# A decoder layer on one core: the third pair of k tiles by seven products in two more stages, and a last group cut further

## The chip, the core and the metric

The kernel runs on one core of one Trainium2 chip, in one launch. The metric is the device time of an execution in microseconds; the times below are medians of three runs. TensorE (PE) does the matmuls, VectorE (DVE) and ScalarE (ACT) the element work, and SyncE (SP) issues the transfers of weights.

## What is computed

One layer of a decoder for 256 tokens and a width of 2048, everything in float32: a gated linear recurrence and an attention side by side, a gated feed-forward block, and a gated embedding at the end. Cut to the products that matter here:

```python
h = rmsnorm(x, g_mix[i])
x_r, g_r, q, k, v, gate_r, gate_a = jnp.split(h @ w_in[i], IN_SPLIT_POINTS, axis=-1)
y_r = (gelu(g_r) * rg_lru(conv(x_r), ...)) @ w_rnn_out[i]
y_a = stick_breaking_attention(norm(q), norm(k), v) @ w_attn_out[i]
x = x + (sigmoid(gate_r) * y_r + sigmoid(gate_a) * y_a) @ w_o[i]
g, u = jnp.split(rmsnorm(x, g_ffn[i]) @ w_ffn_gu[i], 2, axis=-1)
x = x + (silu(g) * u) @ w_ffn_down[i]
ple_gate = sigmoid(rmsnorm(x, g_ple[i]) @ w_ple_gate[i])
x = x + ple_gate * (p[i] @ w_ple_proj[i])
```

The stages that use them are called ro (`w_rnn_out`), v (its columns of `w_in`), ao, wo, gu, dn (`w_ffn_down`, in three parts) and pg (`w_ple_gate`, with `p @ w_ple_proj` inside, which the kernel calls embedded).

## The kernel before

**Products.** Each float32 operand is kept as two parts, hi and lo. A product (`prod`, lines 573 to 575) is three matmuls into one PSUM bank: tokens' hi by weights' hi, hi by lo, lo by hi. The tokens (128 x 128) are what PE loads, 512 columns of weights are what it streams.

**Groups.** The function `group` runs one wide group: 256 tokens by 1024 output columns, as four quarters of 128 tokens by 512 columns, which lie in four PSUM banks called "2", "4", "3" and "8", with a fifth, "B". v and pg have two groups each, g = 0 and 1. A list of slots says what the group does in order. A number is one tile of 128 rows of weights: four products, one for each quarter. Two neighbouring tiles (a pair) can be done with seven products rather than eight, from sums of the four weight blocks and of the token blocks (Strassen's scheme in Winograd's form). The strings "11", "T1", "21", "22", "T2", "T3", "T4" are such slots, and each serves two pairs at a time. `("S", i, 2)`, i from 1 to 4, are the seven products of a third pair. `SEVEN` has two pairs (62 products), `SEVEN3` three (61). Before, only gu uses `SEVEN3`.

**Weights.** `Stream` loads chunks of 512 KB by SP (line 257), plain ones into a ring of four buffers (the profile's w), blocks for sums into Q tiles. SP issues in program order; a plain chunk has to wait until a buffer's wlo has been made. ACT copies the hi part (line 307, whi), DVE subtracts for the lo part (line 308, wlo), chunk by chunk, some four chunks ahead of PE. Where a slot needs a sum, `summed` has DVE add first: a 1024-wide add (line 291) for T1 to T4; for the third pair two 512-wide adds (line 266) for S2 and one each for S3 and S4, which have no transfer of their own.

**Order.** The program is recorded and then put in order by a scheduler, engine by engine, on a simulated timeline. Each engine then runs its instructions in that order and waits on semaphores. Most DVE work is seen in the profile under the helpers' lines: 381 (`tt`, an add or product of two tensors), 384 (`stt`, with a scalar), ACT's under 387 (`actv`).

**Around the change.** The first v group follows the last ro group; its results are read from the banks by DVE and scaled (line 384) while the second v group starts. pg,0 follows the second group of dn's third part, from whose banks DVE adds to the residual x1 (line 381); the sums of squares and the turned tiles (line 1091, small transposes on PE) for the last norm come from these. In the last group (pg,1) the last three k tiles are done quarter by quarter, so that the quarters end one after the other and the gate, the product and the last add run while PE still works; the last quarter's gate is done in two halves of 256 columns.

Of the kernel before, what the change touches and what calls it, by code (L numbers as in the profile page):

```python
# [48 lines left out]
def pairs_of(name):  # L49

    if name[:2] == "dn":
        q = int(name[2])
        return [FQ0[q] // 2 + i for i in range(2 if FQ[q] == 16 else 1)]
    return (0, 1, 2) if name == "gu" else (0, 1)


def is_sum(x):
# [104 lines left out]
def tail():  # L162


    def wide(name, w, slots, c=0):
        return [(name, g, w, c + 8 * g, c + 8 * g + 4, slots[g]) for g in range(2)]

    def blocks(*cs):
        return [("blk", b, None, c, None, None) for c, b in cs]

    def gu(*gs):
        return [("gu", g, "gu", 4 * g, 44 + 4 * g, SEVEN3) for g in gs]

    def dn(q):
        k, p = FQ0[q], FQ0[q] // 2
        slots = [x if isinstance(x, str) else x + k for x in SEVEN] if FQ[q] == 16 else [
            x if isinstance(x, int) else x + (p,) for x in ONE(k)]
        return wide(f"dn{q}", "dn", [slots] * 2)

    x = [("x", 0), ("x", 1)]  # L180
    return (wide("ro", "ro", [LONG] * 2) + wide("v", "in", [SEVEN] * 2, C_V)
            + blocks(*[(c, b) for b in range(4) for c in (C_Q, C_K)], *[(C_GTA, b) for b in range(4)])
            + wide("ao", "ao", [SEVEN] * 2) + wide("wo", "wo", [SEVEN] * 2) + gu(0, 1, 2, 3) + dn(0) + gu(4, 5, 6, 7) + dn(1)
            + gu(8, 9, 10) + dn(2)
            + wide("pg", "pg", [SEVEN[:-3] + x + SEVEN[-3:]] * 2))


HEAD = [("gtr", 0, "in", C_GTR, C_GTR + 4, list(range(KD)))]
# [165 lines left out]
def tile_hybrid_block(ctx: ExitStack, tc: tile.TileContext, xT: bass.AP, x: bass.AP, pT: bass.AP,  # L354
# [285 lines left out]
    def group(at, pairs, sums, after=None, also=()):  # L640
# [6 lines left out]
        name, g = at  # L647
        slots = [x for n, y, _, _, _, sl in HEAD + TAIL if (n, y) == at for x in sl
                 if isinstance(x, int) or is_sum(x)]
        seq = [(n, q) for n, x in enumerate(slots) for q in products(x, pairs_of(name)[:2])]  # L650
        if at == LAST_GROUP:
            k = len(slots) - 3
            rest = [q for q in seq if q[0] >= k]
            seq = [q for q in seq if q[0] < k] + [q for b in "2438" for q in rest if q[1][0] == b]
        first, last = {}, {}
        for i, (_, (b, y, _, _)) in enumerate(seq):
            first.setdefault(b, i)
            last[b] = i
            if y in ("11", "T1", "T2", "T3"):
                last[y] = i  # L660
        plain8 = [i for i, (_, (b, y, _, _)) in enumerate(seq) if b == "8" and not isinstance(y, str)]
        assert "11" not in last or last["T1"] < plain8[0]
        banks, tile_, got = {}, {}, {}
        for i, (n, (b, y, p, c)) in enumerate(seq):
            if n not in got:
                if n in also:
                    also[n]()
# [8 lines left out]
            else:  # L676
# [1 line left out]
                     "T1": sums[p][0], "T2": sums[p][1], "T3": sums[p][2],  # L678
                     "T4": tok(pairs, 2 * p + 1, 1)}[y]
            _, _, hi, lo, w0 = got[n].columns(c)  # L680
            s = slice(w0, w0 + 512)
            prod(ps, o, hi[:, s], lo[:, s], i == first[b], i in (last[b], last.get(y)),
                 b in "B8")
            if y in ("11", "T1", "T2", "T3") and i == last[y]:
                t = tile_[y] = tl("T")
                actv(t, ps, AF.Copy)
                if y == "T2":
                    tt(tile_["T1"], tile_["T1"], t, ALU.subtract)
                if y == "T3" and after is not None:
                    after(tile_)  # L690
        return [banks[b] for b in "2438"], tile_


# [186 lines left out]

    n = len(LONG)
    for g in range(2):
        also = {n - 2 + i: (lambda p: lambda: parts_sums(xg, xsum, p))(p) for i, p in enumerate(pairs_of("v"))} if g else {
            8: last_gate, 12: next_table}
        for i, c in enumerate(whole(("ro", g), y, ysum, also)):
            o = gtr[2 * g + i // 2][i % 2]
            tt(o, c, o, ALU.mult)
# [291 lines left out]
    def embedded(g):  # L1179
        def run():  # L1180
            for b in range(2):
                w_ = S_.take(("tok", "pg", g, ("x", b)))[0]
                for t in range(2):
                    ps = psum()
                    for k in range(2):
                        s = slice(k * 512, k * 512 + 512)
                        prod(ps, tok(pts, k, t), w_[2][:, s], w_[3][:, s], k == 0, k == 1)
                    if g == 0:
                        t_ = tl("T")
                        actv(t_, ps, AF.Copy)  # L1190
                        ps = t_
                    pp.append(ps)
        return run

    for g in range(2):
        qs_, t_ = group(("pg", g), h3, sum3, also={len(SEVEN) - 3: embedded(g)})
        for n, (q, c, op) in enumerate(zip(qs_, ("11", "T3", "T1", "T3"), (ALU.add,) * 3 + (ALU.subtract,))):
            t, b = n % 2, 2 * g + n // 2
            c, ps, o = t_[c], pp.pop(0), tl("T")
            m = 512 if g == 0 or n < 3 else 256  # L1200
            for i in range(0, 512, m):
                s = slice(i, i + m)
                tt(o[:, s], q[:, s], c[:, s], op)
                actv(o[:, s], o[:, s], AF.Sigmoid, scale=rs2[:, t:t + 1])
                tt(o[:, s], ps[:, s], o[:, s], ALU.mult)
                tt(o[:, s], o[:, s], x1[t][b][:, s], ALU.add)
                nc.sync.dma_start(out[t * P:t * P + P, b * 512 + i:b * 512 + i + m], o[:, s])
    assert S_.pos == len(PLAN)


# [59 lines left out]
```

## Time and profile before

| | us |
|---|---|
| median of 3 runs | 1873.09 (1872.94 to 1874.22) |
| the profiled execution | 1875.14 |
| its span in the profile | 1873.4 |
| first v group, first matmul to that of the next | 507.70 to 549.63 |
| second v group, first matmul | 549.86 |
| pg,0, first matmul | 1769.18 |
| pg,1, first matmul to last | 1818.71 to 1866.08 |
| last instruction of DVE ends | 1869.92 |
| SP's wait for the last output ends | 1872.30 |

The span runs from the profiled execution's first instruction to its last; the execution's own time has 1.7 us around it. A row of the timeline gives a start, a length, the engine, the line, the operation, out<-in by the program's names, and in brackets how long the engine stood idle before and what released it. Matmuls overlap in the pipeline, so a matmul is listed with 0.39 us though the next starts 0.227 us after it.

### The profile page before, as it was taken

The numbers are of one execution on the slowest core, as the hardware profiler recorded it, in microseconds if no ns is written. First come the engines' busy times: TensorE is split into PE (matmuls) and PEld (weight loads), VectorE is DVE, ScalarE is ACT, GpSimd is POOL, SyncE is SP. The second block draws the span as 40 slices with busy tenths as digits, with TensorE's granted clock in tenths as the row PEclk, the third lists the DMA queues.
The fourth block names the chain that finished last, engine by engine and source line by source line (L and its number), as shares of the span: only waits on it lengthen the run. The fifth ranks groups of instructions, "written<-read, shape, count | busy, mean of one in ns | idle before, by whom it ended". The sixth has DMA issues, their size and how long they took to land.

```text
span 1873.4 us, 24153 instructions
## 1 busy us (share of the span) xinstructions
PE 1863.6 (99%) x8958; PEld 1567.9 (84%) x8958; DVE 1466.3 (78%) x1777; ACT 1196.1 (64%) x1596; POOL 2.6 (0%) x9
## 2 busy tenths in 40 slices
PE   9999999999999999999999999999999999999998
PEld 7899989888888888888888888888888788888886
DVE  7688887677776576667798988887888888888876
ACT  6688888764555576677555765655556555665773
POOL 0000000000000000000000000000000000000000
PEclk9999999999999999999999999999999999999999
DMA  8556555666546554556466556466454566545554
GB/s 287 179 178 195 191 182 188 239 207 204 196 156 192 192 162 154 165 171 225 146 213 215 196 211 234 166 217 242 166 180 180 180 227 233 197 152 179 189 199 130
DMA packets 101926, 361.37 MB, mean 193 GB/s; under 512 B 11440, under 2 KB 12080, under 8 KB 101808
## 3 DMA queue, kind: packets, MB, share of 16 engines
q1 hardware_dynamic: 101664, 359.82, 56.7%
q8 instruction: 70, 1.15, 0.3%
q14 instruction: 48, 0.39, 0.1%
q10 hardware_dynamic: 144, 0.01, 0.0%
HBM read 357.69 MB, written 2.10 MB: 192 GB/s over the span
## 4 chain that ended last, share of the span: by engine, by line
PE 98%; DMA 1%; DVE 1%; issue 0%; ACT 0%; SPq 0%; DVEq 0%; ACTq 0%
PE ps L574 26%; PE ps L575 26%; PE ps L573 26%; PE ps L503 9%; PE ps L507 4%; PE ps L487 1%; PE ps L486 1%; PE ps L485 1%; PE ps L1149 1%; DMA Q<-in_w_dram 0%; DMA w<-in_w_dram 0%; PE ps L1091 0%; PE ps L930 0%; DVE H L381 0%; DVE wlo L308 0%
## 5 line engine op out<-in xcount | busy, mean ns | idle before, releaser
L308 DVE TENSOR_TENSOR wlo<-w,whi 128x1024 fp32r<-128x1024 f32 (+2 forms) x552 | 666.5, 1214 | 256.0 <-ACT whi L307 251.8
L574 PE MATMUL ps<-wlo,Q 128*128 128x512 f32 x2209 | 861.8, 390 | 0.8 <-DVE wlo L308 0.8
L575 PE MATMUL ps<-whi,Q 128*128 128x512 f32 x2209 | 859.7, 390 | 0.0
L573 PE MATMUL ps<-whi,Q 128*128 128x512 f32 x2209 | 822.1, 391 | 0.0
L307 ACT ACTIVATE whi<-w 128x1024 fp32r<-128x1024 f32 (+2 forms) x552 | 576.0, 1051 | 307.7 <-PE ps L575 259.3
L574 PEld LDWEIGHTS ps<-wlo,Q 128*128 128x128 f32 x2209 | 414.9, 188 | 86.1 <-DVE wlo L308 1.9
L573 PEld LDWEIGHTS ps<-whi,Q 128*128 128x128 f32 x2209 | 414.4, 188 | 86.0 <-ACT H L387 0.5
L575 PEld LDWEIGHTS ps<-whi,Q 128*128 128x128 f32 x2209 | 414.7, 188 | 85.4
L307 ACT ACTIVATE whi<-Q 128x1024 fp32r<-128x1024 f32 (+1 forms) x227 | 234.7, 1036 | 238.3 <-PE ps L575 187.2
L308 DVE TENSOR_TENSOR wlo<-Q,whi 128x1024 fp32r<-128x1024 f32 (+1 forms) x227 | 270.5, 1193 | 60.6 <-ACT whi L307 58.1
L503 PE MATMUL ps<-Q,whi 128*128 128x512 f32 x704 | 170.7, 392 | 0.0
L503 PEld LDWEIGHTS ps<-Q,whi 128*128 128x128 f32 x704 | 128.7, 188 | 24.5
L291 DVE TENSOR_TENSOR Q<-Q,Q 128x1024 f32<-128x1024 f32 x100 | 122.3, 1223 | 6.3 <-DMA Q<-in_w_dram 4.6
L381 DVE TENSOR_TENSOR H<-ps,H 128x512 f32<-128x512 f32 (+1 forms) x158 | 90.3, 603 | 20.4 <-PE ps L575 13.1
L381 DVE TENSOR_TENSOR H<-H,H 128x512 f32<-128x512 f32 (+2 forms) x172 | 100.5, 600 | 7.3 <-ACT H L387 6.8
L387 ACT ACTIVATE H<-ps 128x512 f32<-128x512 f32 (+1 forms) x158 | 81.7, 533 | 37.4 <-PE ps L575 22.5
L507 PEld LDWEIGHTS ps<-Q,wlo 128*128 128x128 f32 x704 | 90.4, 191 | 3.5
L507 PE MATMUL ps<-Q,wlo 128*128 128x256 f32 x704 | 91.5, 283 | 0.0
L387 ACT ACT_TABLE_LOAD x53 | 68.0, 1283 | 1.6 <-DVE Q L381 0.7
L387 ACT ACTIVATE Q<-H 128x512 fp32r<-128x512 f32 x48 | 29.2, 624 | 26.9 <-DVE H L381 26.5
L487 PE MATMUL ps<-Q,wlo 128*128 128x256 f32 x140 | 39.6, 283 | 0.0
L486 PE MATMUL ps<-Q,whi 128*128 128x256 f32 x140 | 39.6, 283 | 0.0
(122 smaller groups left out, 883.1 us busy)
## 6 DMA issues: line engine op xcount, KB each, us to landing
w<-in_w_dram SPq DMA_DIRECT2D x530, 512.0 KB, 4.1
Q<-in_w_dram SPq DMA_DIRECT2D x126, 512.0 KB, 6.1
w<-in_w_dram SPq DMA_DIRECT2D x16, 448.0 KB, 3.4
H<-in_x_dram SPq DMA_DIRECT2D x8, 256.0 KB, 7.0
H<-in_xT_dram SPq DMA_DIRECT2D x7, 256.0 KB, 6.4
out_dram<-H SPq DMA_DIRECT2D x7, 256.0 KB, 2.8
w<-in_w_dram SPq DMA_DIRECT2D x4, 320.0 KB, 3.0
w<-in_w_dram SPq DMA_DIRECT2D x2, 256.0 KB, 3.2
```

What stands on the lines that cost most here:

```text
L291: self.nc.vector.tensor_tensor(r[o], r[o], r[a], ALU.add)
L307: self.hi_ins = self.nc.scalar.activation(hi[:, :c], t[:, :c], AF.Copy)
L308: self.lo_ins = self.nc.vector.tensor_tensor(lo[:, :c], t[:, :c], hi[:, :c].bitcast(F32), ALU.subtract)
L381: nc.vector.tensor_tensor(o, a, b, op)
L387: nc.scalar.activation(o, i, f, **kw)
L486: nc.tensor.matmul(o, wt[0], xl, start=False, stop=False)
L487: nc.tensor.matmul(o, wt[1], xh, start=False, stop=stop)
L503: nc.tensor.matmul(pss[e], wt[0], rhs(xs, k), start=(k == 0), stop=(k == n - 1))
L507: nc.tensor.matmul(pss[e][:, :256], wt[1], rhs(xs, k)[:, :256], start=False, stop=False)
L573: nc.tensor.matmul(ps, x[0], wh, start=start, stop=False, skip_group_check=goes_on)
L574: nc.tensor.matmul(ps, x[0], wl, start=False, stop=False, skip_group_check=goes_on)
L575: nc.tensor.matmul(ps, x[1], wh, start=False, stop=stop, skip_group_check=goes_on)
```

## The change

v and pg take `SEVEN3` instead of `SEVEN`: their third pair of k tiles goes by seven products instead of eight. For v, the token sums of the third pair are made in the last ro group; for pg, `next_h` makes them in the last dn group. In pg,1 the last four k tiles (before: three) go quarter by quarter, and of the last quarter these four tiles go into two new banks, 8a and 8b, of 256 columns each, one after the other; what bank 8 holds from the earlier slots is combined with its correction ahead of that, and each half is added to it. The embedded product's PSUM is copied to SBUF by ACT in both pg groups (before: in the first).

```diff
--- before.py
+++ after.py
@@ -51,7 +51,7 @@
     if name[:2] == "dn":
         q = int(name[2])
         return [FQ0[q] // 2 + i for i in range(2 if FQ[q] == 16 else 1)]
-    return (0, 1, 2) if name == "gu" else (0, 1)
+    return (0, 1, 2) if name in ("gu", "v", "pg") else (0, 1)
 
 
 def is_sum(x):
@@ -178,11 +178,11 @@
         return wide(f"dn{q}", "dn", [slots] * 2)
 
     x = [("x", 0), ("x", 1)]
-    return (wide("ro", "ro", [LONG] * 2) + wide("v", "in", [SEVEN] * 2, C_V)
+    return (wide("ro", "ro", [LONG] * 2) + wide("v", "in", [SEVEN3] * 2, C_V)
             + blocks(*[(c, b) for b in range(4) for c in (C_Q, C_K)], *[(C_GTA, b) for b in range(4)])
             + wide("ao", "ao", [SEVEN] * 2) + wide("wo", "wo", [SEVEN] * 2) + gu(0, 1, 2, 3) + dn(0) + gu(4, 5, 6, 7) + dn(1)
             + gu(8, 9, 10) + dn(2)
-            + wide("pg", "pg", [SEVEN[:-3] + x + SEVEN[-3:]] * 2))
+            + wide("pg", "pg", [SEVEN3[:-4] + x + SEVEN3[-4:]] * 2))
 
 
 HEAD = [("gtr", 0, "in", C_GTR, C_GTR + 4, list(range(KD)))]
@@ -647,21 +647,23 @@
         name, g = at
         slots = [x for n, y, _, _, _, sl in HEAD + TAIL if (n, y) == at for x in sl
                  if isinstance(x, int) or is_sum(x)]
-        seq = [(n, q) for n, x in enumerate(slots) for q in products(x, pairs_of(name)[:2])]
+        seq = [(n, q, 0, 512) for n, x in enumerate(slots) for q in products(x, pairs_of(name)[:2])]
         if at == LAST_GROUP:
-            k = len(slots) - 3
+            k = len(slots) - 4
             rest = [q for q in seq if q[0] >= k]
-            seq = [q for q in seq if q[0] < k] + [q for b in "2438" for q in rest if q[1][0] == b]
+            seq = [q for q in seq if q[0] < k] + [q for b in "243" for q in rest if q[1][0] == b]
+            seq += [(n, (b + f, *q), e, e + 256) for e, f in ((0, "a"), (256, "b")) for n, (b, *q), _, _ in rest
+                    if b == "8"]
         first, last = {}, {}
-        for i, (_, (b, y, _, _)) in enumerate(seq):
+        for i, (_, (b, y, _, _), e, _) in enumerate(seq):
             first.setdefault(b, i)
-            last[b] = i
+            last[b, e] = i
             if y in ("11", "T1", "T2", "T3"):
                 last[y] = i
-        plain8 = [i for i, (_, (b, y, _, _)) in enumerate(seq) if b == "8" and not isinstance(y, str)]
+        plain8 = [i for i, (_, (b, y, _, _), _, _) in enumerate(seq) if b == "8" and not isinstance(y, str)]
         assert "11" not in last or last["T1"] < plain8[0]
         banks, tile_, got = {}, {}, {}
-        for i, (n, (b, y, p, c)) in enumerate(seq):
+        for i, (n, (b, y, p, c), e0, e1) in enumerate(seq):
             if n not in got:
                 if n in also:
                     also[n]()
@@ -678,8 +680,8 @@
                      "T1": sums[p][0], "T2": sums[p][1], "T3": sums[p][2],
                      "T4": tok(pairs, 2 * p + 1, 1)}[y]
             _, _, hi, lo, w0 = got[n].columns(c)
-            s = slice(w0, w0 + 512)
-            prod(ps, o, hi[:, s], lo[:, s], i == first[b], i in (last[b], last.get(y)),
+            s = slice(w0 + e0, w0 + e1)
+            prod(ps[:, e0:e1], o, hi[:, s], lo[:, s], i == first[b], i in (last[b, e0], last.get(y)),
                  b in "B8")
             if y in ("11", "T1", "T2", "T3") and i == last[y]:
                 t = tile_[y] = tl("T")
@@ -688,6 +690,7 @@
                     tt(tile_["T1"], tile_["T1"], t, ALU.subtract)
                 if y == "T3" and after is not None:
                     after(tile_)
+        tile_["ends"] = [banks[b] for b in ("8a", "8b") if b in banks]
         return [banks[b] for b in "2438"], tile_
 
 
@@ -880,7 +883,7 @@
 
     n = len(LONG)
     for g in range(2):
-        also = {n - 2 + i: (lambda p: lambda: parts_sums(xg, xsum, p))(p) for i, p in enumerate(pairs_of("v"))} if g else {
+        also = {n - 3 + i: (lambda p: lambda: parts_sums(xg, xsum, p))(p) for i, p in enumerate(pairs_of("v"))} if g else {
             8: last_gate, 12: next_table}
         for i, c in enumerate(whole(("ro", g), y, ysum, also)):
             o = gtr[2 * g + i // 2][i % 2]
@@ -1185,26 +1188,29 @@
                     for k in range(2):
                         s = slice(k * 512, k * 512 + 512)
                         prod(ps, tok(pts, k, t), w_[2][:, s], w_[3][:, s], k == 0, k == 1)
-                    if g == 0:
-                        t_ = tl("T")
-                        actv(t_, ps, AF.Copy)
-                        ps = t_
-                    pp.append(ps)
+                    t_ = tl("T")
+                    actv(t_, ps, AF.Copy)
+                    pp.append(t_)
         return run
 
     for g in range(2):
-        qs_, t_ = group(("pg", g), h3, sum3, also={len(SEVEN) - 3: embedded(g)})
+        qs_, t_ = group(("pg", g), h3, sum3, also={len(SEVEN3) - 4: embedded(g)})
         for n, (q, c, op) in enumerate(zip(qs_, ("11", "T3", "T1", "T3"), (ALU.add,) * 3 + (ALU.subtract,))):
             t, b = n % 2, 2 * g + n // 2
             c, ps, o = t_[c], pp.pop(0), tl("T")
-            m = 512 if g == 0 or n < 3 else 256
-            for i in range(0, 512, m):
-                s = slice(i, i + m)
-                tt(o[:, s], q[:, s], c[:, s], op)
+            ends = t_["ends"] if n == 3 else []
+            if ends:
+                tt(c, q, c, op)
+            for i in range(0, 512, 256 if ends else 512):
+                s = slice(i, i + 256 if ends else i + 512)
+                if ends:
+                    tt(o[:, s], ends.pop(0)[:, s], c[:, s], ALU.add)
+                else:
+                    tt(o, q, c, op)
                 actv(o[:, s], o[:, s], AF.Sigmoid, scale=rs2[:, t:t + 1])
                 tt(o[:, s], ps[:, s], o[:, s], ALU.mult)
                 tt(o[:, s], o[:, s], x1[t][b][:, s], ALU.add)
-                nc.sync.dma_start(out[t * P:t * P + P, b * 512 + i:b * 512 + i + m], o[:, s])
+                nc.sync.dma_start(out[t * P:t * P + P, b * 512 + s.start:b * 512 + s.stop], o[:, s])
     assert S_.pos == len(PLAN)
```

The order moves at three places. The first is DVE at the beginning of the second v group. A name ending in a number is one tile; H are the first group's results, Q_5184 to Q_5193 what they are scaled into, Q_5199 is the sum for S2, Q_5052 and Q_5079 those for two of the T slots. Before, from the first such eviction that follows PE's end of the first group:

```order
L381 TENSOR_TENSOR H_4987<-ps_4898,H_5039 128x512
L381 TENSOR_TENSOR H_4876<-ps_4902,H_4876 128x512
L384 SCALAR_TENSOR_TENSOR Q_5166<-H_4861,rstd_tok,Q_5166 128x512
L381 TENSOR_TENSOR H_5039<-ps_4863,H_5039 128x512
L308 TENSOR_TENSOR wlo_5180<-w_215_5089,whi_5179 128x1024
L384 SCALAR_TENSOR_TENSOR Q_5169<-H_4987,rstd_tok,Q_5169 128x512
L384 SCALAR_TENSOR_TENSOR Q_5172<-H_4876,rstd_tok,Q_5172 128x512
L308 TENSOR_TENSOR wlo_5195<-Q_5107,whi_5194 128x1024
L384 SCALAR_TENSOR_TENSOR Q_5175<-H_5039,rstd_tok,Q_5175 128x512
L308 TENSOR_TENSOR wlo_5210<-w_217_5126,whi_5209 128x1024
```

and now:

```order
L381 TENSOR_TENSOR H_4956<-ps_4934,H_5050 128x512
L381 TENSOR_TENSOR H_4920<-ps_4938,H_4920 128x512
L384 SCALAR_TENSOR_TENSOR Q_5184<-H_4883,rstd_tok,Q_5184 128x512
L381 TENSOR_TENSOR H_5050<-ps_4889,H_5050 128x512
L384 SCALAR_TENSOR_TENSOR Q_5187<-H_4956,rstd_tok,Q_5187 128x512
L384 SCALAR_TENSOR_TENSOR Q_5190<-H_4920,rstd_tok,Q_5190 128x512
L266 TENSOR_TENSOR Q_5199<-Q_5070,Q_5109 128x512
L384 SCALAR_TENSOR_TENSOR Q_5193<-H_5050,rstd_tok,Q_5193 128x512
L266 TENSOR_TENSOR Q_5199<-Q_5199,Q_5109 128x512
L266 TENSOR_TENSOR Q_5109<-Q_5109 128x512
L291 TENSOR_TENSOR Q_5052<-Q_5052,Q_5197 128x1024
L291 TENSOR_TENSOR Q_5079<-Q_5079,Q_5197 128x1024
```

In the place of the lo parts between and behind the scalings there stand the three 512-wide adds of the third pair and two 1024-wide sums; the lo part of S2 (wlo_5203) and that of tile 6 follow right behind the last row.

The second is SP's queue ahead of pg,0. The Q tiles are the chunks for sums of this group, Q_15159 before and Q_15198 now being "11". Before:

```order
L257 DMA w_736_15131<-in_w_dram 128x1024
L257 DMA w_740_15204<-in_w_dram 128x1024
L257 DMA Q_15159<-in_w_dram 128x1024
L257 DMA Q_15177<-in_w_dram 128x1024
L257 DMA Q_15195<-in_w_dram 128x1024
L257 DMA Q_15240<-in_w_dram 128x1024
L257 DMA w_741_15222<-in_w_dram 128x1024
L257 DMA w_743_15259<-in_w_dram 128x1024
L257 DMA w_744_15277<-in_w_dram 128x1024
```

and now:

```order
L257 DMA w_740_15170<-in_w_dram 128x1024
L257 DMA w_746_15279<-in_w_dram 128x1024
L257 DMA w_748_15314<-in_w_dram 128x1024
L257 DMA w_750_15367<-in_w_dram 128x1024
L257 DMA Q_15198<-in_w_dram 128x1024
L257 DMA Q_15216<-in_w_dram 128x1024
L257 DMA Q_15234<-in_w_dram 128x1024
L257 DMA Q_15243<-in_w_dram 128x1024
L257 DMA Q_15261<-in_w_dram 128x1024
```

The three plain chunks that followed the four Q tiles now stand ahead of them, and the Q tiles are six.

The third is DVE at the beginning of pg,0. H_9182 to H_9188 (before: H_9152 to H_9158) are the residual x1, ps the banks of the last dn group, ssq the sums of squares; Q_15198 and Q_15234 are sums, wlo_15299 belongs to T1, wlo_15317 to 21, Q_15354 and wlo_15358 to S2. Before:

```order
L291 TENSOR_TENSOR Q_15159<-Q_15159,Q_15240 128x1024
L381 TENSOR_TENSOR H_9156<-ps_15039,H_9156 128x512
L308 TENSOR_TENSOR wlo_15280<-w_740_15204,whi_15279 128x1024
L381 TENSOR_TENSOR H_9158<-ps_15007,H_9158 128x512
L308 TENSOR_TENSOR wlo_15316<-w_741_15222,whi_15315 128x1024
L308 TENSOR_TENSOR wlo_15331<-Q_15240,whi_15330 128x1024
L308 TENSOR_TENSOR wlo_15346<-w_743_15259,whi_15345 128x1024
L384 SCALAR_TENSOR_TENSOR Q_15360<-ps_15355,prm_sb,Q_15360 128x256
```

and now:

```order
L266 TENSOR_TENSOR Q_15354<-Q_15216,Q_15261 128x512
L308 TENSOR_TENSOR wlo_15299<-Q_15198,whi_15298 128x1024
L308 TENSOR_TENSOR wlo_15317<-Q_15243,whi_15316 128x1024
L291 TENSOR_TENSOR Q_15234<-Q_15234,Q_15352 128x1024
L266 TENSOR_TENSOR Q_15354<-Q_15354,Q_15261 128x512
L266 TENSOR_TENSOR Q_15261<-Q_15261 128x512
L291 TENSOR_TENSOR Q_15198<-Q_15198,Q_15352 128x1024
L381 TENSOR_TENSOR ssq_8811<-ssq_8811 128x4
L384 SCALAR_TENSOR_TENSOR Q_15399<-ps_15394,prm_sb,Q_15399 128x256
L384 SCALAR_TENSOR_TENSOR Q_15421<-ps_15416,prm_sb,Q_15421 128x256
L384 SCALAR_TENSOR_TENSOR Q_15443<-ps_15438,prm_sb,Q_15443 128x256
L308 TENSOR_TENSOR wlo_15358<-Q_15354,whi_15357 128x1024
```

The adds to x1, of which two stood among these rows, now stand in four rows just ahead of them; three 512-wide adds and one more 1024-wide sum stand ahead of the lo part of S2.

## The prediction

> **What bounds the kernel now.** I read the page first: the busy times, the chain that ended last, the costliest groups.
>
> ```profile
> span 1873.4 us, 24153 instructions
> ...
> PE 1863.6 (99%) x8958; PEld 1567.9 (84%) x8958; DVE 1466.3 (78%) x1777; ACT 1196.1 (64%) x1596; POOL 2.6 (0%) x9
> ...
> PE 98%; DMA 1%; DVE 1%; issue 0%; ACT 0%; SPq 0%; DVEq 0%; ACTq 0%
> ...
> L574 PE MATMUL ps<-wlo,Q 128*128 128x512 f32 x2209 | 861.8, 390 | 0.8 <-DVE wlo L308 0.8
> ```
>
> TensorE is busy for 99% of the span and carries 98% of the chain. The 2209 matmuls of line 574 waited 0.8 us in all, for a wlo that DVE was late with. So a matmul taken out comes off the time, and a tile that comes late goes onto it one for one, as nothing later on PE has slack to give it back. What a matmul is worth I take from the chain, not from the 390 ns of the groups (which overlap):
>
> ```profile
> 169.50 3.65 PE ps L503 x16
> ...
> 200.48 1.91 PE ps L507 x16
> ```
>
> 16 matmuls of 512 columns take 3.65 us, 0.228 each; 16 of 256 columns 1.91, 0.119 each.
>
> The next question is how much room DVE and ACT have where the change puts work, so I read the windows of the stages: the second v group, a gate-up group (these run with three pairs already), the end of the third down projection, the first pg group.
>
> ```profile
> core 0: us, PE busy (x) PEld busy (x) DVE busy (x) ACT busy (x) POOL busy (x), PEclk, DMA share, GB/s
> 549.90:591.90 42.00, 42.00 (x187) 34.80 (x186) 29.28 (x29) 24.22 (x27) 0.00 (x0) 1.00 0.58 185
> 1108.10:1150.50 42.40, 42.40 (x192) 35.10 (x192) 37.74 (x40) 26.39 (x31) 0.00 (x0) 1.00 0.55 199
> 1735.30:1769.00 33.70, 33.70 (x158) 27.89 (x157) 28.43 (x43) 23.57 (x39) 0.00 (x0) 1.00 0.59 205
> 1769.20:1818.60 49.40, 49.40 (x227) 40.88 (x226) 38.07 (x42) 35.20 (x48) 0.00 (x0) 1.00 0.55 192
> ```
>
> The gate-up group has DVE busy for 37.74 of 42.40 us and PE without a gap: three pairs can be fed on the mean. The mean does not settle it, since a group needs its sums in its first 10 us, where DVE also empties the banks of the group before.
>
> **What is taken out.** Four groups (v and pg, two each) go from 62 to 61 products of three matmuls: 4 x 3 = 12 matmuls of 512 columns, 12 x 0.228 = **-2.74 us**. It counts in full, as PE has no gaps.
>
> **v, second group.** The sums of the third pair are new here: S2 takes two 512-wide adds (line 266), S3 one, and DVE runs in program order. By the order they now stand behind the evictions and the scalings of the first v group's results, and behind them stand two 1024-wide sums (line 291), and only then the wlo of S2. How long these take I read from the same place before:
>
> ```profile
> 549.76 1.28 DVE L381 TENSOR_TENSOR H<-ps,H 128x512 f32<-128x512 f32 x2
> 550.96 0.74 DVE L384 SCALAR_TENSOR_TENSOR Q<-H,rstd_tok,Q 128x512 fp32r<-128x512 f32 x1
> 551.62 0.69 DVE L381 TENSOR_TENSOR H<-ps,H 128x512 f32<-128x512 f32 x1
> 552.22 1.22 DVE L308 TENSOR_TENSOR wlo<-w,whi 128x1024 fp32r<-128x1024 f32 x1
> 553.35 1.41 DVE L384 SCALAR_TENSOR_TENSOR Q<-H,rstd_tok,Q 128x512 fp32r<-128x512 f32 x2
> ...
> 562.56 1.22 DVE L291 TENSOR_TENSOR Q<-Q,Q 128x1024 f32<-128x1024 f32 x1
> 563.69 1.22 DVE L308 TENSOR_TENSOR wlo<-w,whi 128x1024 fp32r<-128x1024 f32 x1
> ```
>
> From start to start: an add of 512 columns 0.60, a scaling (line 384) 0.66, a wlo 1.13, a 1024-wide sum 1.13. The first eviction at 549.76 waits for PE's last matmuls of the first group, so it cannot move. From it, in the new order, up to the wlo of S2: three evictions and four scalings (3 x 0.60 + 4 x 0.66), three 512-wide adds (1.80), two 1024-wide sums (2.26), together 8.50 us. That wlo starts at 549.76 + 8.50 = 558.26 and ends 1.22 later, 559.48. On PE the first matmul that reads it stands, in the order, 29 matmuls of 512 columns behind the group's start at 549.86: 549.86 + 29 x 0.227 = 556.44 (0.227 is what the matmuls of such a group are apart, within 1% of the 0.228). So PE must wait **3.0 us** here. (ACT's whi of S2, 1.05 us, comes behind the second add and is late too, by less.) What is queued behind on PE is the whole rest of the kernel.
>
> **v, first group.** There the adds of S2 stand ahead of the group's start, and by the same pitches wlo of S2 is ready 2.4 us before it is read. At nothing; covered by PE's matmuls on the slots ahead. Were that cover gone, it would cost as much as in the second group. The token sums of the third pair (in the last ro group for v, in dn2 for pg, a handful of short DVE adds each) lie beside PE in the same way.
>
> **pg, first group.** Here the order moves DMAs too. The chunks for sums of this group ("11" first) were issued ahead of three plain chunks on SP's queue, and now stand behind three such:
>
> ```profile
> 1754.01 1.85 SPq L257 DMA_DIRECT2D Q<-in_w_dram  x4
> 1757.38 2.60 SPq L257 DMA_DIRECT2D w<-in_w_dram  x3
> ```
>
> and for how long these 13 transfers took:
>
> ```profile
> DMA to landing us min/median/max: 3.5/6.2/8.7
> ```
>
> Such a plain chunk must wait until a wlo has freed its buffer, which at this place let the three out between 1757.38 and 1757.38 + 2.60 = 1759.98. So "11" is issued at about 1759.6 and not at 1754.01, and lands, with a landing of 4.3 us (between the least and the median of that row, as fewer transfers are queued ahead), at 1763.9. Behind it ACT's whi (1.05), then DVE goes without a gap through the order's rows: from wlo of "11" at 1765.0 to the wlo of S2 there are four wlo (4.52), three 1024-wide sums (3.39), four evictions of dn2 and three 512-wide adds (7 x 0.60 = 4.20), three scalings of 256 columns (1.2, by half of line 384's width and its fixed part) and small ones: 13.6 us. The wlo of S2 starts at 1778.6 and ends at 1779.8. On PE its reader is 29 matmuls of 512 columns and 12 small transposes behind the group's start:
>
> ```profile
> 1769.18 0.39 PE L573 MATMUL ps<-whi,Q 128*128 128x512 f32 x1
> ...
> 1774.42 0.60 PE L1091 MATMUL ps<-ident,H 128*128 128x128 f32 x4
> 1774.78 0.47 PE L574 MATMUL ps<-wlo,Q 128*128 128x512 f32 x1
> ```
>
> Four transposes move the next matmul by 0.36, 0.09 each. So it is wanted at 1769.18 + 6.58 + 1.08 = 1776.84, and PE waits **2.9 us**. From below: if "11" landed as early as before, the four evictions of dn2 would hold the row back instead, as the last of them follows PE's end of dn2 at 1769.2; from there nine rows (8.5 us) and the wlo make 1778.9, a wait of 2.1. From above: with the 8.7 us of the same row everything is 4.4 later, a wait of 7.3.
>
> **pg, second group.** Its S2 adds stand early (2.3 us after the group's start the wlo is under way, wanted 6.6 after it). At nothing.
>
> **Starting again after a wait.** The one wait of this profile shows it:
>
> ```profile
> 1494.20 0.39 PE L573 MATMUL ps<-whi,Q 128*128 128x512 f32 x1
> 1495.38 0.50 PE L574 MATMUL ps<-wlo,Q 128*128 128x512 f32 x1 [0.79 <-DVE wlo L308]
> 1495.72 0.40 PE L575 MATMUL ps<-whi,Q 128*128 128x512 f32 x1
> 1496.14 0.51 PE L573 MATMUL ps<-whi,Q 128*128 128x512 f32 x1
> 1496.49 0.40 PE L574 MATMUL ps<-wlo,Q 128*128 128x512 f32 x1
> 1496.72 0.40 PE L575 MATMUL ps<-whi,Q 128*128 128x512 f32 x1
> ```
>
> Without a wait the matmul of 1495.38 starts at 1494.43, and four matmuls later one starts at 1495.34; it started at 1496.72. Of 1.38 us, 0.95 are the wait and 0.43 the three slow matmuls behind it. I charge 0.45 for each of the two places, **+0.9**; the bounds are 0 and 1 (v's wait falls into three pieces).
>
> On the same rows a rule of the Trainium skill bears, "TensorE: Matmul & The Clock Gate", "Part 1: The HAM clock gate": after an idle window of about 3.4 us the clock is halved, and it is a busy window of that length that brings it back. The 0.79 us wait left the granted clock at 1.00 in its stage, as the rule would have it; no run here shows a longer one.
>
> **Last quarter and tail.** 12 matmuls of 512 columns become 24 of 256: 24 x 0.119 - 12 x 0.228 = +0.13, and the last one starts 0.25 later and, being half as wide, ends a little earlier. Behind it before:
>
> ```profile
> 1866.08 0.39 PE L575 MATMUL ps<-whi,Q 128*128 128x512 f32 x1
> ...
> 1866.51 1.69 DVE L381 TENSOR_TENSOR H<-ps,H 128x256 f32<-128x256 f32 x4 [0.67 <-PE ps L575]
> ...
> 1868.11 1.02 DVE L381 TENSOR_TENSOR H<-H,H 128x512 f32<-128x512 f32 x2
> 1869.04 0.42 DVE L381 TENSOR_TENSOR H<-ps,H 128x256 f32<-128x256 f32 x1
> 1869.49 0.42 DVE L381 TENSOR_TENSOR H<-H,H 128x256 f32<-128x256 f32 x1
> ```
>
> Seven DVE operations follow, the last ends 3.83 after the last matmul's start. Now the first half's operations and the subtraction stand ahead of it; but four k tiles by quarters let quarters 2 and 4 end within 0.5 us of each other, so DVE is full and takes the second half's add 0.7 after that start (before 0.43); with the same operations behind it I come to 3.17, 0.67 less. Together 0.25 - 0.67 = **-0.4**, between -0.7 (DVE in time) and 0. The four PSUM copies that ACT now makes for the embedding lie where ACT is busy for 35.20 of 49.40 us; at nothing.
>
> **The sum:** -2.74 + 3.0 + 2.9 + 0.9 - 0.4 = **+3.7 us**. The profiled execution took 1875.14 (span 1873.4 and 1.7 around it), 2.05 above the median; the sum is a difference made on its rows and stands on the median: 1873.09 + 3.7 = **1876.8**.
>
> **The rivals.**
>
> - *One wait is hidden.* DVE's evictions or the DMA of pg come earlier than I lay them. The window of dn2's end is for it (DVE 28.43 of 33.70 us, so some gaps); the eviction that waits for PE at 549.76 is against it for v. One wait with its restart less: +0.2 to +0.4, 1873.4.
> - *The change does what it says.* Gate-up runs 11 groups with three pairs and no wait of PE. Then -2.74 - 0.4 = -3.1: 1870.0. Against it: there the S2 adds stand well ahead of their use, here in two groups they do not.
> - *pg's first chunk lands late.* If "11" takes as long as the slowest of its neighbours, 8.7 us, PE waits 7.3 and not 2.9: 1881.2, slower. It counts from the point at which "11" lands later than 1763.9, each us of it one us. Against it: the queue ahead of it is shorter by the time it is issued.
> - *The clock falls in the wait.* If the matmuls behind each wait ran at twice 0.228 for as long as the wait of 3 us lasted, each loses 1.5 more: 1879.8. The section on the clock gate named above would bring this about, at an idle window of 3.4 us. Against it: both waits are in pieces below 2.5 us with matmuls between.
>
> **How the numbers follow.** The forecast as summed gets 0.60 (1875.2 to 1878.4, by the restart's and the tail's bounds and pg's wait of 2.1), one wait hidden 0.15, what it says 0.09, the late landing 0.12 (between 1878 and 1881.2), the clock 0.04. The range leaves out the case that it does what it says and the upper part of the last two: 1873.0 to 1880.0. About 0.2%, 3.7 us, is what a measurement of this kernel can tell from no change: faster is below 1869.35, slower above 1876.83. The forecast lies on that edge and gives half to each: slower 0.31 + 0.12 + 0.04 = 0.47, the same 0.29 + 0.15 + 0.05 = 0.49, faster 0.04, from the lower part of that case alone.
>
> **What would show it.** Line 574's idle time before it should grow from 0.8 us to some 5 to 6, for wlo of line 308, with two places: 6 to 8 us into the second v group, and as far into the first pg group; lines 573 and 575 should show whi's. The windows of v's first group should shrink by 0.7 us, its second's grow by 2.7. If PE shows no wait in v's second group, my order of DVE there is not what decides; if the wait at pg is above 4, look when "11" landed; if the matmuls after a wait are slow for microseconds, it was the clock. If the last output leaves more than 3.6 us after PE's last start, the tail term was wrong.

## The result, and the profile after

The changed kernel takes 1878.14 us (median of 8 runs, 1876.92 to 1881.90); the kernel before, in 8 runs, 1873.39 (1872.94 to 1874.22). The ratio is 1.0027, with a 95% interval from 1.0016 to 1.0038: slower by 4.75 us, where 3.7 were forecast. The page of the changed kernel (busy time, chain, the matmul groups with their idle time):

```profile
span 1877.7 us, 24205 instructions
...
PE 1863.9 (99%) x8958; PEld 1567.0 (83%) x8958; DVE 1484.9 (79%) x1812; ACT 1206.0 (64%) x1611; POOL 2.6 (0%) x9
...
PE 96%; DVE 2%; DMA 1%; issue 0%; ACT 0%; SPq 0%; ACTq 0%
...
L574 PE MATMUL ps<-wlo,Q 128*128 128x512 f32 (+1 forms) x2209 | 861.8, 390 | 2.2 <-DVE wlo L308 2.2
...
L573 PE MATMUL ps<-whi,Q 128*128 128x512 f32 (+1 forms) x2209 | 817.2, 391 | 3.1 <-ACT whi L307 3.1
```

PE now stands idle for 2.2 us ahead of line 574 and 3.1 ahead of line 573, 5.3 in place of 0.8, and DVE has grown from 1% to 2% of the chain. Both places that the prediction named are there. PE's timeline in the second v group (start, length, and in brackets the idle time and its releaser):

```profile
554.17 0.39 PE L575 MATMUL ps<-whi,Q 128*128 128x512 f32 x1
555.80 0.73 PE L573 MATMUL ps<-whi,Q 128*128 128x512 f32 x2 [1.24 <-ACT whi L307]
556.75 0.96 PE L573 MATMUL ps<-whi,Q 128*128 128x512 f32 x3 [0.22 <-ACT whi L307]
558.66 0.50 PE L574 MATMUL ps<-wlo,Q 128*128 128x512 f32 x1 [0.95 <-DVE wlo L308]
559.00 0.40 PE L575 MATMUL ps<-whi,Q 128*128 128x512 f32 x1
```

and in the first pg group:

```profile
1776.61 0.39 PE L575 MATMUL ps<-whi,Q 128*128 128x512 f32 x1
1778.41 0.73 PE L573 MATMUL ps<-whi,Q 128*128 128x512 f32 x2 [1.41 <-ACT whi L307]
1779.36 0.97 PE L573 MATMUL ps<-whi,Q 128*128 128x512 f32 x3 [0.22 <-ACT whi L307]
1781.38 0.69 PE L574 MATMUL ps<-wlo,Q 128*128 128x512 f32 x1 [1.05 <-DVE wlo L308]
1781.87 0.63 PE L575 MATMUL ps<-whi,Q 128*128 128x512 f32 x1
1782.30 0.63 PE L574 MATMUL ps<-wlo,Q 128*128 128x512 f32 x1
```

The two waits look alike: S2's whi, tile 6's whi, S2's wlo. What follows differs. In v the next matmuls start 0.24 us apart, in pg 0.43. Nine of them do, and the windows view says why (the eighth column, ahead of the DMA share and GB/s, is the granted clock):

```profile
core 0: us, PE busy (x) PEld busy (x) DVE busy (x) ACT busy (x) POOL busy (x), PEclk, DMA share, GB/s
...
554.50:558.60 4.10, 1.75 (x6) 0.78 (x5) 4.10 (x6) 3.91 (x5) 0.00 (x0) 1.00 0.00 0
558.60:562.40 3.80, 3.74 (x16) 3.03 (x17) 3.80 (x5) 2.39 (x3) 0.00 (x0) 1.00 0.27 108
...
1777.00:1781.40 4.40, 1.72 (x7) 0.80 (x6) 4.40 (x10) 4.10 (x5) 0.00 (x0) 1.00 0.00 0
1781.40:1784.90 3.50, 3.50 (x9) 2.72 (x10) 3.50 (x4) 3.47 (x7) 0.00 (x0) 0.52 0.27 101
```

Behind the wait in pg the clock was 0.52 for 3.5 us, with 9 matmuls where some 15 belong; behind the one in v it was 1.00.

Laying the first matmul of each stage of one profiled execution against the other gives the whole of the 4.3 us between the spans: 0.2 less at the start; -0.68 in the first v group (three matmuls, as forecast); +2.65 in the second; -1.38 in the first group of dn's second part; +4.87 in pg,0; -0.42 in pg,1; -0.5 behind the last matmul. The -1.38 is not the change's: the wait at 1494.59, quoted in the prediction, was not there this time. Its chunk had landed 8.2 us after its issue and now 6.9; of the runs below only pg alone has a wait there again (1.10 us).

### The profile page after: what moved, and what is told of

It is laid out like the page before. It is cut to its first block, busy times and chain, and to the rows that moved or that the text cites. A ratio compares the mean times of both kernels' runs of the same rounds, so it can differ in the third digit from the quotient of the medians.

```text
span 1877.7 us, 24205 instructions
## 1 busy us (share of the span) xinstructions
PE 1863.9 (99%) x8958; PEld 1567.0 (83%) x8958; DVE 1484.9 (79%) x1812; ACT 1206.0 (64%) x1611; POOL 2.6 (0%) x9
## 4 chain that ended last, share of the span: by engine, by line
PE 96%; DVE 2%; DMA 1%; issue 0%; ACT 0%; SPq 0%; ACTq 0%
PE ps L574 26%; PE ps L575 26%; PE ps L573 26%; PE ps L503 9%; PE ps L507 4%; PE ps L487 1%; PE ps L486 1%; PE ps L485 1%; DVE H L381 1%; DVE wlo L308 1%; PE ps L1152 1%; PE ps L933 0%; DMA Q<-in_w_dram 0%; DVE Q L291 0%; DMA w<-in_w_dram 0%; PE ps L1094 0%
## 5 line engine op out<-in xcount | busy, mean ns | idle before, releaser
L574 PE MATMUL ps<-wlo,Q 128*128 128x512 f32 (+1 forms) x2209 | 861.8, 390 | 2.2 <-DVE wlo L308 2.2
L575 PE MATMUL ps<-whi,Q 128*128 128x512 f32 (+1 forms) x2209 | 859.6, 390 | 0.0
L308 DVE TENSOR_TENSOR wlo<-w,whi 128x1024 fp32r<-128x1024 f32 (+2 forms) x544 | 656.5, 1213 | 241.3 <-ACT whi L307 235.1
L573 PE MATMUL ps<-whi,Q 128*128 128x512 f32 (+1 forms) x2209 | 817.2, 391 | 3.1 <-ACT whi L307 3.1
L307 ACT ACTIVATE whi<-w 128x1024 fp32r<-128x1024 f32 (+2 forms) x544 | 567.7, 1051 | 286.9 <-PE ps L575 235.2
L307 ACT ACTIVATE whi<-Q 128x1024 fp32r<-128x1024 f32 (+1 forms) x243 | 249.9, 1030 | 251.4 <-PE ps L575 204.7
L308 DVE TENSOR_TENSOR wlo<-Q,whi 128x1024 fp32r<-128x1024 f32 (+1 forms) x243 | 287.4, 1185 | 64.6 <-ACT whi L307 62.1
```

Source lines behind the costliest of these rows:

```text
L307: self.hi_ins = self.nc.scalar.activation(hi[:, :c], t[:, :c], AF.Copy)
L308: self.lo_ins = self.nc.vector.tensor_tensor(lo[:, :c], t[:, :c], hi[:, :c].bitcast(F32), ALU.subtract)
L573: nc.tensor.matmul(ps, x[0], wh, start=start, stop=False, skip_group_check=goes_on)
L574: nc.tensor.matmul(ps, x[0], wl, start=False, stop=False, skip_group_check=goes_on)
L575: nc.tensor.matmul(ps, x[1], wh, start=False, stop=stop, skip_group_check=goes_on)
```

## Experiments

Seven kernels take the change apart or mend one of its waits, one makes a wait longer, two put together what held. The times of the kernel before that each is compared with were taken on the same chip beside them: 1873.99 (the first four), 1873.98 (the next four), 1873.90 (the last two). "Loss" below is the time of one group, from its first matmul to the next group's, above what its matmuls took before, the matmuls saved taken into account: 3.3 us for v's second group in the changed kernel (2.65 + 0.68), 5.55 for pg,0 (4.87 + 0.68). For v's second group the first matmuls are at 549.86 and 592.02 before, at 548.96 and 593.77 now; for pg,0 and pg,1 at 1769.18 and 1818.71 before, at 1769.58 and 1823.97 now. (In the table of the profile before, 549.63 is the start of the first v group's last matmul; the next group's first is at 549.86.)

### v alone

```diff
-    return (0, 1, 2) if name == "gu" else (0, 1)
+    return (0, 1, 2) if name in ("gu", "v") else (0, 1)
...
-wide("v", "in", [SEVEN] * 2, C_V)
+wide("v", "in", [SEVEN3] * 2, C_V)
```

> Three pairs in v alone, pg and the last group as before. Theory (DVE's order at the start of the second v group): the two v groups save 6 matmuls, -1.36 us, and PE waits for the whi and wlo of S2 as in the changed kernel, 3.3 us with the restart: +2.0, about 1875.3 us. Rival (the wait in v belongs to the changed kernel as a whole, or the loss sits in pg alone): no wait in the second v group, -1.4, about 1872.0.

1875.67 us, ratio 1.0010 (1.0001 to 1.0019): 1.7 above before, as the theory has it. The profiled execution says more. Its windows around the wait in v:

```profile
555.00:559.10 4.10, 1.74 (x6) 0.78 (x5) 4.10 (x6) 3.93 (x5) 0.00 (x0) 1.00 0.00 0
559.10:562.90 3.80, 3.76 (x10) 2.95 (x11) 3.80 (x4) 2.57 (x3) 0.00 (x0) 0.55 0.37 108
```

PE's idle pieces are those of the changed kernel to 0.01 us (1.24, 0.22, 0.94), PE is busy for 1.74 of 4.10 us as there, and yet here the clock falls to 0.55 for the 3.8 us behind them; the loss is 4.87 and not 3.3. So the wait belongs to v, and whether the clock falls behind it changes from execution to execution. The times agree: the three longest of the ten runs (1876.82 to 1877.49) have a mean granted clock of 0.998, the seven others (1874.62 to 1875.83) 0.999.

### pg alone

```diff
-    return (0, 1, 2) if name == "gu" else (0, 1)
+    return (0, 1, 2) if name in ("gu", "pg") else (0, 1)
...
-            + wide("pg", "pg", [SEVEN[:-3] + x + SEVEN[-3:]] * 2))
+            + wide("pg", "pg", [SEVEN3[:-3] + x + SEVEN3[-3:]] * 2))
```

> Three pairs in pg alone, v and the last three tiles by quarters as before. Theory (chunk 11 of pg,0 issued behind three plain chunks, so that S2's lo part is some 4 us late): -1.36, +4.1 of wait, and +1.8 where the granted clock falls to half for a window of 3.5 us behind the wait: +2.7 or +4.5, 1876.1 to 1877.9 us. Rival (the wait in pg comes from v's change or from the last group): no wait, about 1872.0.

1878.82 us (1876.49 to 1881.04), ratio 1.0025 (1.0014 to 1.0036): 4.8 above before, 0.3 more than the dearer of the theory's two cases. In the profiled execution the loss in pg,0 is 7.2 us (6.49 and 0.68): chunk 11 was issued at 1759.60 and landed 6.4 us later, and the clock fell again, here already before the last piece of the wait:

```profile
1777.20:1782.00 4.80, 2.73 (x7) 1.05 (x6) 4.80 (x11) 4.06 (x5) 0.00 (x0) 0.80 0.00 0
1782.00:1786.70 4.70, 4.67 (x11) 3.75 (x12) 4.70 (x6) 4.65 (x8) 0.00 (x0) 0.50 0.41 123
```

The wait in pg is pg's own.

### The last group alone

v and pg with two pairs, the four last tiles by quarters and the two banks as in the change. Against the changed kernel:

```diff
-    return (0, 1, 2) if name in ("gu", "v", "pg") else (0, 1)
+    return (0, 1, 2) if name == "gu" else (0, 1)
...
-[SEVEN3[:-4] + x + SEVEN3[-4:]] * 2
+[SEVEN[:-4] + x + SEVEN[-4:]] * 2
```

> Only the last group is cut further (four tiles by quarters, the last quarter in two banks), v and pg with two pairs. Theory: the last matmul starts 0.25 us later and the tail behind it is 0.7 shorter: -0.4, about 1873.0 us. Rival (DVE is too full at the end for it): 0 to +0.5, 1873.4 to 1873.9.

1873.15 us, ratio 0.9995 (0.9986 to 1.0005). It is on the theory's side, but the interval does not tell it from nothing. The traces say more. In this run's own the last matmul starts at 1865.03 and the last operation of DVE ends at 1867.88, 2.85 later, where it was 3.83 before. In the changed kernel the tail gains less. DVE at its end:

```profile
1870.81 0.42 DVE L381 TENSOR_TENSOR H<-ps,H 128x256 f32<-128x256 f32 x1
1871.14 0.68 DVE L381 TENSOR_TENSOR H<-H,H 128x512 f32<-128x512 f32 x1
1871.74 0.42 DVE L381 TENSOR_TENSOR H<-ps,H 128x256 f32<-128x256 f32 x1
1872.08 2.15 DVE L381 TENSOR_TENSOR H<-H,H 128x256 f32<-128x256 f32 x5
```

The last matmul starts at 1870.92; the last operation ends at 1872.08 + 2.15 = 1874.23, 3.31 later, where 3.17 were forecast. DVE has no gap over 0.03 us in it: it is DVE, not PE, that the second half waits for.

### Early chunks for pg,0

```diff
-EARLY = {("ro", 0): 4}
+EARLY = {("ro", 0): 4, ("pg", 0): 4}
```

> The changed kernel, with the chunks for sums of pg,0 put four places earlier in the order of the weight transfers. Theory (the landing of 11 sets the row of DVE at pg,0): 11 lands some 5 us or more earlier, then the four adds to x1, which follow PE's end of dn2, hold the row: a wait of about 2 instead of 4.1 and no half clock, so 2 to 4 us less than the changed kernel: 1874 to 1876. Rival (DVE's own work is the bound at pg,0 whatever lands): no gain, 1878.

1876.16 us, ratio 1.0012 (1.0003 to 1.0022): 2.6 less above before than the changed kernel's 4.75. The loss in pg,0 falls from 5.55 to 1.4 us, and the clock stays up; v, untouched, has the same idle pieces as ever (1.23, 0.22, 0.95), and this time no fall of the clock:

```profile
554.80:558.90 4.10, 1.74 (x6) 0.78 (x5) 4.10 (x6) 3.93 (x5) 0.00 (x0) 1.00 0.00 0
558.90:562.70 3.80, 3.76 (x16) 3.04 (x17) 3.80 (x4) 2.35 (x3) 0.00 (x0) 1.00 0.34 99
...
1776.40:1779.20 2.80, 2.60 (x10) 1.61 (x9) 2.80 (x5) 2.80 (x9) 0.00 (x0) 1.00 0.00 0
```

So the greater part of pg's wait comes from when its chunks are issued and land. The run does not separate the landing from DVE's order, which the scheduler laid anew for it: the four adds to x1 now come two and two (1770.56 and 1774.09).

### The sums held in program order

DVE's adds for the sums of v and pg are ordered behind the lo part that precedes them in the program, so that no sum of a later slot overtakes S2's lo part. `issue_after` adds such an edge for the scheduler, on DVE alone.

```diff
+            if is_sum(mode) and PLAN[i][0][1] in ("v", "pg"):
+                with self.tc.issue_after(self.lo_ins.ins):
+                    t, c = self.summed(mode)
```

> The changed kernel, with the sums of v and pg held on DVE behind the lo part that precedes them in the program, so that S2's lo part no longer stands behind two sums of later slots. Theory (DVE's row decides): in v the wait for S2's lo falls from 3.1 to 1.4, then one for T2 of 0.4; in pg from 4.1 to about 1.4, with the same late landing of 11: 3 to 5 us less than the changed kernel, about 1874.5. Rival (the wait comes from the late chunks and ACT's hi parts, whatever DVE's order): no gain, 1878.

1882.31 us, ratio 1.0045 (1.0029 to 1.0060): 8.3 above before, and the expectation was wrong. In pg,0 the loss fell, from 5.55 to 2.95, and the clock stayed up. In v's second group only the wait for S2's lo part is gone: the pieces of 1.24 and 0.21 for the hi parts of S2 and tile 6 stay, one of 0.45 for tile 7's hi part is new, and the group still lost 2.85. In pg,0 the largest piece is now 1.47, for ACT's copy of a bank, which stands behind two loads of an activation table (ACT_TABLE_LOAD, 1.28 us each). And the other two groups, which the changed kernel runs without a wait, lost 1.3 and 3.1. PE in pg,0 and in pg,1 (the lines are four further on here: 577 is tokens' hi by weights' hi, 578 hi by lo):

```profile
1783.15 0.50 PE L577 MATMUL ps<-whi,Q 128*128 128x512 f32 x1 [1.47 <-ACT H L390]
...
1830.13 0.50 PE L578 MATMUL ps<-wlo,Q 128*128 128x512 f32 x1 [1.03 <-DVE wlo L311]
```

The early sums are no mistake of the order as such. They were in the way in two places; held back, they cost the other two groups more (4.4 us) than they gave in these (3.1).

### The scalings later

The four scalings of the first v group's results are recorded in the second group, behind T2's lo part.

```diff
+    v0 = whole(("v", 0), xg, xsum)
+    def scaled_v0():
+        with behind_splits():
+            scaled_v(v0)
+    scaled_v(whole(("v", 1), xg, xsum, {3: scaled_v0}))
```

> The changed kernel, with the four scalings of the first v group's results put behind T2's lo part in the second v group. Theory: these 2.65 us of DVE stand ahead of S2's lo part; without them it is ready when PE asks for it: no wait in v, 3.3 less (more where the clock had fallen there): 1874.8, pg as in the changed kernel. Rival (the evictions or the sums hold it): the wait in v stays, 1878.

1877.17 us (1875.36 to 1878.44), ratio 1.0016 (1.0007 to 1.0025). In the profiled execution PE has no idle time at all in v's second group, and both v groups are 0.68 shorter than before, so that v's loss of 3.3 is gone whole:

```profile
549.30:559.00 9.70, 9.70 (x44) 8.02 (x44) 9.70 (x14) 9.12 (x12) 0.95 (x1) 1.00 0.16 54
...
1773.90:1778.50 4.60, 1.93 (x6) 0.79 (x5) 4.60 (x10) 4.05 (x5) 0.00 (x0) 0.87 0.00 0
1778.50:1784.20 5.70, 5.67 (x13) 4.46 (x14) 5.70 (x8) 5.64 (x10) 0.00 (x0) 0.50 0.42 146
```

DVE's order at this place is what v waited for. But the edit moved more than the four scalings. The scheduler now put S2's two adds 49 us earlier, ahead of the whole first v group, and its lo part right behind the evictions:

```profile
503.27 0.68 DVE L266 TENSOR_TENSOR Q<-Q,Q 128x512 f32<-128x512 f32 x1
...
505.01 0.68 DVE L266 TENSOR_TENSOR Q<-Q,Q 128x512 f32<-128x512 f32 x1
...
551.17 1.22 DVE L308 TENSOR_TENSOR wlo<-Q,whi 128x1024 fp32r<-128x1024 f32 x1
```

That lo part starts at 551.17 and not at 557.38, and the scalings' 2.65 us are less than half of the 6.2 between. ACT's part of the scalings moved with them; in the changed kernel ACT stood idle for 2.28 us ahead of S2's hi part, until DVE's second add was done. So the row as a whole decides; what the scalings alone do this run does not show.

Above before the kernel stands by 3.2 in place of 4.75, so the median gained 1.6 and not 3.3: in the profiled execution pg,0, unmended, lost 6.65, its clock at half for 6.8 us. Most of its runs had such a fall: the mean granted clock is 0.997 or 0.998 in nine of the ten, and 0.999 or 1.000 in all 15 of the kernel before.

### All three edits

The changed kernel with the three diffs above (early chunks, sums in order, scalings later) together:

```diff
+EARLY = {("ro", 0): 4, ("pg", 0): 4}
...
+                with self.tc.issue_after(self.lo_ins.ins):
...
+    scaled_v(whole(("v", 1), xg, xsum, {3: scaled_v0}))
```

> The changed kernel with all three edits: early chunks for pg,0, sums in order, scalings later. Theory: no wait of over 0.5 us in either group and no half clock, so that the 12 matmuls and the shorter tail are kept: 3.1 less than before, about 1870.5 us. Rival (a new wait takes the place of the old one, at a later slot): 1872 to 1874.

1882.20 us, ratio 1.0041 (1.0028 to 1.0053): the rival, and worse than it. As with the sums in order alone, v's first group (+1.3) and pg,1 wait, v's second group still loses 2.5 us and pg,0 2.8. The sums in order undo what the other two edits gain.

### A longer wait

Four more 512-wide adds on DVE, that write S2's sum in the second v group again, ahead of its whi.

```diff
                 add(y[:, 512:], y[:, :512], b[:, :512])
+                if PLAN[self.at][0][1:3] == ("v", 1):
+                    for _ in range(4):
+                        add(y[:, 512:], y[:, :512], b[:, :512])
```

> The changed kernel with four more 512-wide adds on DVE ahead of the hi part of S2 in the second v group (they write the same sum again). By the order PE's first wait there grows from 1.2 to some 5 us in one piece, and the wait in all by 3.6. Theory (an idle of this length always lets the clock fall): the granted clock is about 0.5 for some 3.5 us behind it and the time is 3.6 + 1.7 = 5.3 above the changed kernel, 1883.4. Rival (the clock falls only by chance or for other reasons): +3.6 and a clock of 1.00, 1881.7.

1885.93 us (1884.18 to 1887.04), 12.0 above before, so 7.2 more than the changed kernel's 4.75, and more than either theory. PE's wait came in one piece of 6.88 us, and behind it:

```profile
554.90:561.80 6.90, 0.02 (x2) 0.01 (x1) 5.62 (x9) 1.11 (x2) 0.00 (x0) 0.87 0.00 0
561.80:566.80 5.00, 5.00 (x12) 3.68 (x13) 5.00 (x5) 4.88 (x6) 0.95 (x1) 0.50 0.31 79
```

The clock was at half for the 5 us behind the wait, and already within its last part. The group lost 9.57: some 7.05 of wait and 2.5 of clock (half of 5.0 us). All four runs have a mean granted clock of 0.996 or 0.997.

### What holds, put together

Two kernels. The first has three pairs in both v groups, with the scalings later, and in the last pg group, with the change's tail, and two pairs in the first pg group:

```diff
-            + wide("pg", "pg", [SEVEN3[:-4] + x + SEVEN3[-4:]] * 2))
+            + wide("pg", "pg", [SEVEN[:-4] + x + SEVEN[-4:], SEVEN3[:-4] + x + SEVEN3[-4:]]))
```

> Three pairs where their sums come in time: both v groups, with the scalings of the first put later, and the last pg group, with the change's tail; the first pg group keeps two pairs. Theory: 9 matmuls less, -2.05, the tail -0.4, no wait and no half clock: 2.4 less than before, about 1871.5 us. Rival (pg,0 waits all the same, since dn2 makes the third pair's token sums in front of it): 1873 to 1875.

1872.52 us (1870.81 to 1873.55), ratio 0.9991 (0.9982 to 1.0000), between the theory and the rival. PE waits for no weights at all in the profiled execution, the fastest of its runs:

```profile
L574 PE MATMUL ps<-wlo,Q 128*128 128x512 f32 (+1 forms) x2210 | 861.1, 390 | 0.0
L575 PE MATMUL ps<-whi,Q 128*128 128x512 f32 (+1 forms) x2210 | 859.1, 389 | 0.0
L573 PE MATMUL ps<-whi,Q 128*128 128x512 f32 (+1 forms) x2210 | 813.3, 391 | 0.0
```

The second is the changed kernel with the scalings later and the early chunks:

```diff
+EARLY = {("ro", 0): 4, ("pg", 0): 4}
...
+    scaled_v(whole(("v", 1), xg, xsum, {3: scaled_v0}))
```

> The changed kernel with the scalings later and the early chunks for pg,0, without the sums in order. Theory: v without a wait, pg,0 with waits of 1.4 in all as the run with early chunks had: -2.74 - 0.4 + 1.4 = 1.7 less than before, about 1872.2 us. Rival (the clock still falls at pg,0 by chance, or the two edits disturb each other): 1874 to 1876.

1872.08 us (1871.81 to 1872.85), ratio 0.9990 (0.9981 to 0.9999). It keeps one wait of 0.65 us in pg,0, where it loses 1.7. Both are 1.4 to 1.8 below the kernel before and about 6 below the changed one; that is at the edge of what the intervals can tell from no gain over the kernel before.

## Why the prediction came out as it did

The time lay in the range and on the side forecast, by the mechanism forecast. By its steps:

- **The matmuls taken out**, -2.74: measured as -0.68 in each group that runs undisturbed. Right.
- **The wait in v's second group**, 3.0 and 0.45 to start again: 3.33 in the profiled execution, with the rows as laid (S2's wlo ends 9.64 us after the group's start, forecast 9.62):

```profile
555.11 2.35 DVE L291 TENSOR_TENSOR Q<-Q,Q 128x1024 f32<-128x1024 f32 x2
557.38 1.22 DVE L308 TENSOR_TENSOR wlo<-Q,whi 128x1024 fp32r<-128x1024 f32 x1
```

  That DVE's order is the cause is shown by the run with the scalings later, where PE does not wait. Right.
- **The wait in pg,0**, 2.9 and 0.45: 5.55 in all. The step that was mis-sized is the landing. The six chunks were issued when forecast, behind the three plain ones, but "11" took 5.5 us and not 4.3 (1765.39; 1764.3 forecast, with the 0.4 by which the stage began later). SP's queue, the first of the six by itself, and DVE behind it:

```profile
1759.90 3.08 SPq L257 DMA_DIRECT2D Q<-in_w_dram  x6
...
L257 SPq DMA_DIRECT2D Q<-in_w_dram x1: 425/425/425, 1759.9 to 1759.9; - x1
...
DMA to landing us min/median/max: 5.5/5.5/5.5
...
1766.56 2.51 DVE L308 TENSOR_TENSOR wlo<-Q,whi 128x1024 fp32r<-128x1024 f32 x2 [2.51 <-ACT whi L307]
```

  DVE stood idle for 2.51 us for it, and S2's wlo came 1.1 later than laid. The rival of the late landing so came in part, 1.1 us of its 4.4. The run with early chunks, which takes the loss to 1.4, fits that. Of the 5.55, some 3.85 are wait and 1.7 the half clock (half of 3.4 us).
- **The clock** was given 4 chances in 100, on the ground that both waits are in pieces below 2.5 us. That reason was wrong: the longest piece in pg,0 was 1.41, and the clock fell; what counted was the idle time summed over a window of 3.4 us (last section). The price (1.5 for each wait) was about right.
- **Starting again**, 0.45: where the clock stayed up, in v, the first wlo matmul of S2 took 0.34 to the next, 0.1 more than its share; the 0.43 seen before was too much.
- **Tail**, -0.4: +0.26 to the last matmul's start and -0.52 behind it, -0.26. Right within its bounds.
- **Not in the sum**: the 1.4 that the kernel before had lost to a late chunk in its profiled execution. It is in that execution's time, 1875.14, and not in a median of 1873.39. Setting the difference on the median was right, but the difference of two single executions (4.3) holds this chance too.

By the groups the change cost 5.9 us in the profiled execution (-0.68 + 2.65 + 4.87 - 0.42 - 0.5), some 4.2 without the half clock, against 3.7 summed. The median's 4.75 lies between, and it does not need the clock: two of the eight runs have a mean granted clock of 1.000, which leaves no room for 3.4 us at half (0.0009 of the span), and they took 1877.99 and 1878.05. The longest, 1881.90, has 0.997. So the later landing is the part of the miss that the traces show; how much of the rest varies from run to run is open, as only one run has a profile.

## What to carry to other kernels

A saving of matmuls counts only where the operands of the first slots are ready: lay out the rows of the engine that makes them, from the last event that can't move to the first use, before trusting a busy share of 70 to 80%. Where a wait of some 3 us is unavoidable in a kernel that PE bounds, allow for about 1.7 us more (half of the 3.4 us that the clock was at half here), even if the wait comes in pieces. And of edits that mend an order, try each alone: the one that held all sums in order undid two that were sound.

## What the runs showed of the hardware

The granted clock falls behind waits that are not of one piece, and the windows that decide it lie on a fixed grid. The same idle pieces of 1.24, 0.22 and 0.95 us, to 0.01 us, left it at 1.00 in two profiled executions (the changed kernel, the early chunks) and brought it to half in one (v alone). Each spell of half clock inside a kernel lasted 3.41 us (the changed kernel, v alone) or twice that (pg alone, scalings later). The kernel with the longer wait has two spells, from 559.98 and from 1788.78, and the 1228.80 us between them are 360 times 3.413. Cut at the bounds of this grid, the rows around the waits are these, of the changed kernel (v, then pg,0), of v alone and of the early chunks (v):

```profile
552.73:556.15 3.42, 2.18 (x11) 1.47 (x9) 3.42 (x5) 1.46 (x2) 0.00 (x0) 1.00 0.00 0
556.15:559.56 3.41, 2.24 (x9) 1.24 (x8) 3.41 (x4) 3.41 (x5) 0.00 (x0) 1.00 0.00 0
1778.12:1781.53 3.41, 1.85 (x6) 0.93 (x7) 3.41 (x8) 3.41 (x5) 0.00 (x0) 1.00 0.00 0
1781.53:1784.94 3.41, 3.41 (x9) 2.63 (x10) 3.41 (x4) 3.38 (x7) 0.00 (x0) 0.50 0.30 109
...
555.96:559.37 3.41, 1.93 (x6) 1.02 (x7) 3.41 (x4) 3.41 (x5) 0.00 (x0) 1.00 0.00 0
559.37:562.78 3.41, 3.41 (x9) 2.63 (x9) 3.41 (x4) 2.30 (x3) 0.00 (x0) 0.50 0.37 102
...
554.27:557.69 3.42, 1.97 (x8) 0.94 (x6) 3.42 (x6) 2.72 (x3) 0.00 (x0) 1.00 0.00 0
```

In v of the changed kernel the bound splits the pieces into 1.24 and 1.17 us of idle time, and the clock stayed up; in v alone 1.48 fell into one window, and it was at half from that window's end. The windows ahead of the other falls had 1.56 (pg,0 above), 1.62 (pg alone), 1.67 (scalings later), 1.71 and 3.41 (the longer wait). Among those with no fall behind them the early chunks had 1.45, and one row does not fit: in the longer wait's group the window from 553.16 had 1.66, all at its end, and the clock fell a window later. So about 1.5 us of idle time in such a window of 3.41 was enough here; the border is not shown more closely, as the ends of matmuls are modelled.

The Trainium skill, "TensorE: Matmul & The Clock Gate", "Part 1: The HAM clock gate", tells of a window of 3.4 us that runs freely, not started by the kernel, after which the clock is halved if PE was idle. The half clock, the 3.41 us and the grid agree. But PE was busy for 1.85 of the 3.41 us ahead of the fall in pg,0, so an idle share of the window, not an idle window, was enough.
